# Attention's values in two passes over one bank, its sums on GpSimd, in a hybrid encoder layer

## The chip, the cores and the metric

The kernel runs on one core of one Trainium2 chip, in one launch. The metric is the device time of that launch in microseconds.

## The reference

One encoder layer is applied to two sequences of 2048 and 256 positions with the same weights. All inputs are fp32. Cut to what matters here:

```python
def encoder_layer(x, ...):
    h = rmsnorm(x, norm1_w)
    mq, mk, mv, mo, gates, aq, ak, av = jnp.split(h @ w_in, cuts, axis=-1)
    m_out = mlstm_mixer(mq, mk, mv, mo, gates, b_gates, mh_norm_w)   # 8 heads of 64, both directions
    a_out = attention_mixer(aq, ak, av, q_norm_w, k_norm_w)          # 8 query heads, 2 key/value heads
    x = x + jnp.concatenate([m_out, a_out], axis=-1) @ w_out
    u = centred_dwconv(rmsnorm(x, norm2_w) @ w_up, conv_w, conv_b)
    a, g = jnp.split(u, 2, axis=-1)
    return x + (jax.nn.silu(g) * a) @ w_down

# within attention_mixer, after the rms norms of q and k and the rotary embedding:
    def block(qi):
        s = jnp.einsum('bqhgd,bkhd->bhgqk', qi, k).astype(jnp.float32) * scale
        p = jax.nn.softmax(s, axis=-1)
        return jnp.einsum('bhgqk,bkhd->bqhgd', p.astype(v.dtype), v)
```

## The kernel before

Matrix products on fp32 data are made from fp32r products, TensorE's rounded form of fp32: an operand x is split into a high part (x rounded to fp32r) and a low part (x minus the high part, rounded again), and a product is high x high + high x low + low x high. `g.ident`, `g.identr` and `g.ones` are an identity in fp32, one in fp32r and a 128x2 block of ones.

**Stages.** `phase_a` normalises the input and projects gates, queries, keys and values of attention. `gate_math` prepares the mLSTM's gates. Then `run_both` interleaves two generators, `attention` and `mlstm`, step by step: each step yields its estimated TensorE time, and the one that is behind in its share goes next (`A_PAIR`, `A_MAX` and `A_PREP` are the estimates of attention's steps). When the mLSTM is through, the rest of attention is interleaved with `phase_c`, the output projection, and `phase_d`, the feed-forward part, follows. Within a stage a planner orders each engine's instructions by a simulated schedule and by priorities; the mLSTM's small steps have a high one. Each engine then works through its own list in order.

**Attention.** The work is cut into 36 query groups of 512 columns (four blocks of 128 queries; one head or two). 32 groups see the 2048 keys of the long sequence, that is 16 blocks of 128 keys, and 4 see the 256 keys of the short one, 2 blocks. In all there are 32 x 16 + 4 x 2 = 520 blocks of 128 keys by 512 queries. One step `kp` takes two such blocks:

- `scores`: two fp32r matmuls (lines 595 and 596) put the scores, with the query's maximum already taken off, into a PSUM bank `ps`. ScalarE takes exp twice: once rounded to fp32r into `ph` (line 599), and once in fp32 back into the bank (line 600). VectorE subtracts them into the low part `pl` (line 601).
- `maxstep`: for the next group, a matmul of queries against 512 keys into a bank `px` (line 569), of which VectorE takes the maximum per query (line 570). The banks of `ps`, `px` and a few transposes are the four buffers of the tag `sc`.
- `values`, two steps later (`PLAG`): six matmuls of line 613 add to the bank `pv`. The high values lie in a tile with 64 columns of ones beside them, so that the products of `ph` and `pl` with them leave the values on partitions 0 to 63 and the sums of the exps, 64 times over, on partitions 64 to 127. The low values lie in a tile of 64 columns, whose product with `ph` goes to partitions 0 to 63 alone.

At the end of a group `fin1` copies both halves of `pv` out with ScalarE (lines 621 and 622). The list `fins` holds what follows, of which one entry is done per step: `fin2` four times (VectorE inverts a quarter of the 64x512 sums, line 630), `fin3` (GpSimd multiplies, line 634, and issues the stores to `mix_d`), `fin4` (marks rows as ready for `phase_c`).

**What else runs on GpSimd in this stretch**, in its one queue: the mLSTM's mask selects (line 864) behind their loads (line 856), its weighted keys (line 825), the powers of its rms norms (lines 100 and 101), and in `phase_c` the sums of squares (line 1054). Other operations that the prediction names: line 849 (the mLSTM's recurrence), 904 to 921 (its outputs), 1029 (split of the mixed heads in `phase_c`), 131 and 142 (the sums of squares over partitions and their broadcast over columns, in `rstd_cols` and `rstd_rows`), and in `phase_d` 1181, 1278, 1364 and 1374 on VectorE and 1189 to 1192 on GpSimd.

Of the kernel before, what the change touches and what calls it, by code (L numbers as in the profile page):

```python
# [9 lines left out]
F32 = mybir.dt.float32  # L10
F32R = mybir.dt.float32r
AF = mybir.ActivationFunctionType
ALU = mybir.AluOpType
# [4 lines left out]
P = 128  # L18
# [6 lines left out]
HD = 64  # L25
# [32 lines left out]
DMB = 6  # L58
KWB = 2
LEAD = 1.3  # L60
A_PAIR = 2.3
A_MAX = 0.23
A_PREP = 1.0
C_MM = 1.43
# [8 lines left out]
PO = 4  # L73
PB = 4
PHB = 6
PLB = 6
PLAG = 2
ZT = 3
SG = 3
# [9 lines left out]
def f32(ap):  # L89
    return ap.bitcast(F32)  # L90
# [382 lines left out]
def attention(g, tc, s1, s2, pp):  # L473


    nc = g.nc
    sp = s1
# [13 lines left out]
    def load_kv(grp, k0, k1, after=None):  # L491

        if (grp, k0) in kv:
            return
        n = k1 - k0
        sp = s2 if n == NT1 else s1
        kv[(grp, k0)] = parts = []
        for t0 in range(0, n, 4):
            m = min(4, n - t0)
            s = f"{n}_{t0}"  # L500
            kk = sp.tile([P, m * P], F32R, tag="kk" + s, name=f"kk{grp}_{s}", bufs=1)
            kl1 = sp.tile([65, m * P], F32R, tag="kl1" + s, name=f"kl1{grp}_{s}", bufs=1)
            vs = [sp.tile([P, m, P if a == 0 else HD], F32R, tag=f"v{a}" + s, name=f"v{a}{grp}_{s}", bufs=1)
                  for a in range(2)]
            c = slice((k0 + t0) * P, (k0 + t0 + m) * P)
            if after is not None:
                for t in (kk[0:1, 0:1], kk[HD:HD + 1, 0:1], kl1[0:1, 0:1], vs[0][0:1, 0, 0:1], vs[1][0:1, 0, 0:1]):
                    nc.gpsimd.tensor_copy(t, after[0:1, 0:1])
            nc.gpsimd.memset(f32(vs[0][:, :, HD:]), 1.0)
            for r in (0, HD):  # L510
                nc.gpsimd.dma_start(f32(kk[r:r + HD, :]), g.k_d[grp, 0:HD, c])
            nc.gpsimd.dma_start(f32(kl1[0:HD, :]), g.k_d[grp, HD:P, c])
            nc.gpsimd.memset(f32(kl1[64:65, :]), 1.0)
            for a in range(2):
                nc.gpsimd.dma_start(f32(vs[a][:, :, 0:HD]), g.v_d[a, grp, :, k0 + t0:k0 + t0 + m])
            parts.append((kk, kl1, vs))

    class HB:
        pass
# [1 line left out]
    def part(s):  # L521

        t, r = 0, []
        for q in s.qs:
            r.append((t, q))
            t += q[2] - q[1]
        return r
# [13 lines left out]
    def prep(n):  # L541

        s = HB()
        grp, s.qs, k0, k1 = hbs[n]
        load_q(n)
        load_q(n + 1)
        load_kv(grp, k0, k1)
        s.kv = kv[(grp, k0)]
        s.nq, s.nk = 4, k1 - k0
        s.N = s.nq * P  # L550
        s.nm = "%d_%d" % s.qs[0][0:2]
        qz = qzs.pop(n)
# [35 lines left out]
    def scores(s, kp):  # L588
        N = s.N
        parts = []  # L590
        for z in range(2):
            ps = pp.tile([P, 512], F32, tag="sc", name=f"ps{s.nm}_{kp}_{z}")[:, 0:N]
            kk, kl1, _ = s.kv[kp // 2]
            kc = (2 * kp + z) % 4 * P
            nc.tensor.matmul(ps, kk[:, kc:kc + P], s.qq[:, 0:N], start=True, stop=False)  # L595
            nc.tensor.matmul(ps, kl1[:, kc:kc + P], s.qm[:, 0:N], start=False, stop=True)  # L596
            ph, pl = (sp.tile([P, 512], F32R, tag=t, name=f"{t}{s.nm}_{kp}_{z}", bufs=n)[:, 0:N]
                      for t, n in (("ph", PHB), ("pl", PLB)))
            nc.scalar.activation(ph, ps, AF.Exp)  # L599
            nc.scalar.activation(ps, ps, AF.Exp)  # L600
            nc.vector.tensor_tensor(pl, ps, f32(ph), ALU.subtract)  # L601
            parts.append((ph, pl))
        return parts

    def values(s, kp, parts):

        N = s.N
        if kp == 0:
            s.pv = pp.tile([P, 512], F32, tag="pv", name="pv" + s.nm, bufs=1)
        vs = [[v[:, (2 * kp + z) % 4, :] for v in s.kv[kp // 2][2]] for z in range(2)]  # L610
        todo = [(vs[z][k], parts[z][0]) for z in range(2) for k in range(2)] + [(vs[z][0], parts[z][1]) for z in range(2)]
        for k, (v, p) in enumerate(todo):
            nc.tensor.matmul(s.pv[0:HD if k in (1, 3) else P, 0:N], v, p, start=(kp == 0 and k == 0),  # L613
                             stop=(2 * kp + 2 == s.nk and k == 5))

    def fin1(s):

        N = s.N
        s.o1 = sp.tile([HD, 512], F32, tag="o1", name="o1" + s.nm, bufs=2)
        s.rs = sp.tile([HD, 512], F32, tag="rs", name="rs" + s.nm, bufs=1)  # L620
        nc.scalar.activation(s.o1[:, 0:N], s.pv[0:HD, 0:N], AF.Copy)
        nc.scalar.activation(s.rs[:, 0:N], s.pv[HD:P, 0:N], AF.Copy)
        s.left = list(range(0, N, P))

    def fin2(s):

        if s.left:
            r = s.rs[:, s.left[0]:s.left[0] + P]
            s.left.pop(0)
            nc.vector.reciprocal(r, r)  # L630

    def fin3(s):
        N = s.N
        nc.gpsimd.tensor_tensor(s.o1[:, 0:N], s.o1[:, 0:N], s.rs[:, 0:N], ALU.mult)
        for t0, (h, q0, q1) in part(s):
            r0 = HD * (h % 2)
            nc.gpsimd.dma_start(g.mix_d[q0 // 2:q1 // 2, r0:r0 + HD, 4 + h // 2].rearrange("n p t -> p n t"),
                                s.o1[:, t0 * P:(t0 + q1 - q0) * P].rearrange("p (n t) -> p n t", t=BT))
# [15 lines left out]
    prep2a(cur)  # L654
    prep2b(cur)
    load_kv(0, 0, NT1, cur.m4)
    todo, fins = [], []

    def value():

        s, kp, parts = todo.pop(0)
        values(s, kp, parts)
        if kp == s.nk // 2 - 1:
            while fins:
                fins.pop(0)()
            fin1(s)
            fins.extend([lambda: fin2(s)] * 4 + [lambda: fin3(s), lambda: fin4(s)])

    for n in range(len(hbs)):
        nxt = prep(n + 1) if n + 1 < len(hbs) else None  # L670
# [3 lines left out]
        for kp in range(nkp):  # L674
            todo.append((cur, kp, scores(cur, kp)))
            yield 0.4 * A_PAIR
            if ready:
                prep2b(ready)
                ready = None
            if nxt is not None and nxt.todo:  # L680
                if n == len(hbs) // 2 - 1:

                    k = 2 * (kp - 2) - (nxt.nq * nxt.nsp - len(nxt.todo))
                else:
                    k = -(-len(nxt.todo) // max(nkp - kp - (MXZ if g.alone else MXE), 1))
                for i in range(k):
                    maxstep(nxt)
                    if i % 2:
                        yield 2 * A_MAX
                if not nxt.todo:  # L690
                    prep2a(nxt)
                    ready = nxt
            if len(todo) > PLAG:
                value()
                yield 0.6 * A_PAIR
            for _ in range(1 if kp < nkp - 1 else 2):
                if fins:
                    fins.pop(0)()
# [9 lines left out]
    while todo:  # L708
        yield A_PAIR
        value()  # L710
# [873 lines left out]
```

## Time and profile before

| | |
|---|---|
| device time, median of 3 runs | 3426.95 us (3423.08 to 3429.48) |
| the profiled execution, first to last instruction | 3427.2 us |
| TensorE busy | 3329.3 us, 97% |
| VectorE busy | 2677.3 us, 78% |
| ScalarE busy | 1931.2 us, 56% |
| GpSimd busy | 1120.9 us, 33% |

The profiled execution's time is its span; nothing is recorded outside it, and it stands 0.25 us over the median of the runs. In the profile's lines PE is TensorE's matmuls, PEld its weight loads, DVE VectorE, ACT ScalarE and POOL GpSimd; a line number such as L601 is one of the kernel before.

How to read them: a group of instructions is given as line, engine, operation, output<-inputs, shapes and count, then the busy time in us and the mean of one in ns, then the idle time of that engine just before them and what ended it. An answer in order of time gives start and length in us, then engine, line and operation; several like instructions in a row are merged into one line (x4). A row of a stretch of time gives its bounds and length, then the busy time of each engine with its count in brackets, TensorE's granted clock, the share of the DMA engines and GB/s; asked for one source line, it has that line's busy time alone. A row of waits names who waited, for whom, the sum in us, how often, and the longest.

### The profile page before, as it was taken

The numbers are of one execution on the slowest core, as the hardware profiler recorded it, in microseconds if no ns is written. First come the engines' busy times: TensorE is split into PE (matmuls) and PEld (weight loads), VectorE is DVE, ScalarE is ACT, GpSimd is POOL, SyncE is SP. The second block draws the span as 40 slices with busy tenths as digits, with TensorE's granted clock in tenths as the row PEclk, the third lists the DMA queues.
The fourth block names the chain that finished last, engine by engine and source line by source line (L and its number), as shares of the span: only waits on it lengthen the run. The fifth ranks groups of instructions, "written<-read, shape, count | busy, mean of one in ns | idle before, by whom it ended". The sixth has DMA issues, their size and how long they took to land. (4 is left out here: it accounts for less than half of the span.)

```text
span 3427.2 us, 55596 instructions
## 1 busy us (share of the span) xinstructions
PE 3329.3 (97%) x20058; PEld 3098.4 (90%) x20058; DVE 2677.3 (78%) x4654; ACT 1931.2 (56%) x4329; POOL 1120.9 (33%) x1328
## 2 busy tenths in 40 slices
PE   7989999999999999899999999999999999999998
PEld 6878888888888888688899999999999999999998
DVE  6885687777768788967767878789888888888776
ACT  4536666666666767655544444446444446555554
POOL 6653132213232323211244333226233224322222
PEclk9999999999999999999999999999999999999999
DMA  6765342333345444422365232223323213421221
GB/s 220 243 203 159 89 140 86 115 123 98 108 131 160 143 123 139 145 77 94 101 216 198 81 105 87 68 80 133 129 94 103 72 59 128 140 74 62 69 74 50
DMA packets 254756, 404.27 MB, mean 118 GB/s; under 512 B 32112, under 2 KB 156816, under 8 KB 254480
## 3 DMA queue, kind: packets, MB, share of 16 engines
q1 hardware_dynamic: 226576, 358.23, 32.7%
q0 software_dynamic: 11344, 33.04, 3.6%
q10 hardware_dynamic: 16560, 9.44, 0.9%
q8 instruction: 158, 2.59, 0.3%
q14 instruction: 118, 0.97, 0.1%
HBM read 316.73 MB, written 83.90 MB: 117 GB/s over the span
## 5 line engine op out<-in xcount | busy, mean ns | idle before, releaser
L1322 PE MATMUL pd<-act,wd 128*128 128x384 f32 (+1 forms) x3120 | 593.4, 336 | 23.9 <-DVE acc L1324 12.6
L1322 PEld LDWEIGHTS pd<-act,wd 128*128 128x128 f32 x3120 | 539.6, 188 | 32.6 <-DVE acc L1324 18.1
L601 DVE TENSOR_TENSOR pl<-ps,ph 128x512 fp32r<-128x512 f32 x520 | 352.7, 683 | 181.5 <-ACT ps L600 173.4
L1184 PE MATMUL pa<-nt,wut 128*128 128x386 f32 (+2 forms) x2376 | 454.3, 339 | 0.0
L599 ACT ACTIVATE ph<-ps 128x512 fp32r<-128x512 f32 x520 | 309.4, 595 | 243.5 <-PE ps L596 239.5
L1184 PEld LDWEIGHTS pa<-nt,wut 128*128 128x128 f32 x2376 | 421.6, 190 | 0.3 <-ACT u L1200 0.3
L570 DVE TENSOR_REDUCE mx<-px 128x1 f32<-128x512 f32 (+1 forms) x528 | 345.5, 670 | 74.4 <-PE px L569 72.4
L1278 DVE SCALAR_TENSOR_TENSOR y<-u,cw,y 128x768 f32<-128x768 f32 (+1 forms) x264 | 315.6, 1196 | 36.4 <-ACT y L1271 29.3
L1189 POOL TENSOR_TENSOR tw<-ru 128x512 f32<-128x512 f32 x66 | 94.1, 1425 | 732.5 <-DMA ru<-w_up 558.5
L613 PE MATMUL pv<-ph,v 128*128 128x512 f32 (+1 forms) x1040 | 319.4, 401 | 1.0 <-ACT ph L599 0.8
L600 ACT ACTIVATE ps<-ps 128x512 f32<-128x512 f32 x520 | 310.3, 597 | 0.0
L1200 ACT ACTIVATE u<-pa 128x386 f32<-128x386 f32 (+2 forms) x264 | 128.3, 486 | 320.9 <-PE pa L1184 320.7
L1324 DVE TENSOR_TENSOR acc<-pd,acc 128x384 f32<-128x384 f32 (+1 forms) x544 | 280.3, 535 | 35.5 <-PE pd L1322 34.1
L1041 PEld LDWEIGHTS po<-cmx,wo 128*128 128x128 f32 x1728 | 220.7, 191 | 8.2 <-DVE mmx L931 0.6
L1041 PE MATMUL po<-cmx,wo 128*128 128x256 f32 x1728 | 224.2, 284 | 0.4 <-DVE mmx L931 0.4
L595 PE MATMUL ps<-qq,kk 128*128 128x512 f32 x520 | 215.5, 416 | 4.2 <-DVE mx L570 2.4
L569 PE MATMUL px<-kk,qq 128*128 128x512 f32 (+1 forms) x528 | 202.8, 413 | 6.0 <-DVE mx L570 2.9
L596 PE MATMUL ps<-qm,kl 65*128 65x512 f32 x520 | 206.7, 399 | 0.0
L759 PE MATMUL mj<-mn,wm 128*128 128x256 f32 x1296 | 203.0, 289 | 2.8 <-ACT og L773 1.9
L759 PEld LDWEIGHTS mj<-mn,wm 128*128 128x128 f32 x1296 | 187.1, 193 | 19.8 <-ACT og L773 2.0
L769 PEld LDWEIGHTS mv<-wm,mn 128*128 128x128 f32 x1296 | 182.8, 190 | 18.4 <-ACT qb L765 2.5
L769 PE MATMUL mv<-wm,mn 128*128 128x256 f32 x1296 | 196.5, 285 | 1.0 <-ACT qb L765 0.9
(288 smaller groups left out, 7266.6 us busy)
## 6 DMA issues: line engine op xcount, KB each, us to landing
ru<-w_up SPq DMA_DIRECT2D x132, 512.0 KB, 3.4
mn<-n_d SPq DMA_DIRECT2D x216, 256.0 KB, 3.4
rd<-w_down SPq DMA_DIRECT2D x66, 512.0 KB, 3.6
n_d<-n1T SPq DMA_DIRECT2D x18, 1024.0 KB, 5.6
dm<-nm_d POOLq DMA_DIRECT2D x72, 256.0 KB, 4.1
mjn<-n_d SPq DMA_DIRECT2D x72, 256.0 KB, 3.3
mvn<-n_d SPq DMA_DIRECT2D x72, 256.0 KB, 3.1
q_d<-qz SPq DMA_DIRECT2D x18, 512.0 KB, 3.7
```

The source lines that it names most:

```text
L570: nc.vector.tensor_reduce(s.mx[:, t, z0:z0 + 1], ps[:, 0:w], AX.X, ALU.max)
L599: nc.scalar.activation(ph, ps, AF.Exp)
L600: nc.scalar.activation(ps, ps, AF.Exp)
L601: nc.vector.tensor_tensor(pl, ps, f32(ph), ALU.subtract)
L613: nc.tensor.matmul(s.pv[0:HD if k in (1, 3) else P, 0:N], v, p, start=(kp == 0 and k == 0), stop=(2 * kp + 2 == s.nk and k == 5))
L759: nc.tensor.matmul(pj[:, o], s.w[c][:, a, o * P:(o + 1) * P], nT[c][:, :, h, :], start=(c + o + k == 0), stop=(c == NCC - 1 and k == 2 and ...
L769: nc.tensor.matmul(pv[:, o], nT[c][:, o, a, :], s.w[c][:, h, 256:512], start=(c + o + k == 0), stop=(c == NCC - 1 and k == 2 and o == 1))
L1041: nc.tensor.matmul(po[:, o], wo[z // 2][c][:, a, n], mx[c][:, h, :], start=(c == 0 and k == 0), stop=(c == NCC - 1 and k == 2))
L1184: nc.tensor.matmul(p, w[:, aa, c, :], ops[k][:, c, bb, 0:n], start=c == 0 and i == 0 and not add, stop=c == NCC // 2 - 1 and i == 2, skip_ ...
L1278: nc.vector.scalar_tensor_tensor(y[:, s:e], u[:, s + k:e + k], cw[:, k, jj:jj + 1], y[:, s:e], ALU.mult, ALU.add)
L1322: nc.tensor.matmul(po, wds[j][c // 4][:, aa, c % 4 * P:(c % 4 + 1) * P], acts[j][:, bb, z0:z1], start=(j == 0 and k == 0), stop=(j == len( ...
L1324: nc.vector.tensor_tensor(accs[c][:, z0:z1], po, accs[c][:, z0:z1], ALU.add)
```

## The change

The low values move beside the high ones, into the place of the ones: one tile `v` with the high values in columns 64 to 127 and the low ones in columns 0 to 63. A block's values are then two matmuls, of `ph` and of `pl`, both with all 128 columns: the bank gets the products with the low values on partitions 0 to 63 and with the high values on 64 to 127, and `fin1` adds the two halves (a copy of one on ScalarE, an addition on VectorE). The product low x low is now included.

The sums of the exps are no longer made on TensorE. The fp32 exp goes to a tile `pf` in SBUF (three buffers) instead of back into the bank; VectorE subtracts from there, and GpSimd adds the blocks of a group up in `acc`. At the end, `fin1b` sums `acc` over partitions with four fp32 matmuls by two columns of ones, so that the sums stand as columns, and inverts these; `fin2` broadcasts them back to rows with four fp32 matmuls through the identity, and ScalarE copies them out. The buffers of `pl` go from 6 to 5 and those of `o1` from 2 to 1, and the estimate `A_PAIR` from 2.3 to 1.9.

```diff
-A_PAIR = 2.3
+A_PAIR = 1.9
-PLB = 6
+PLB = 5
+PFB = 3
...
-            vs = [sp.tile([P, m, P if a == 0 else HD], F32R, tag=f"v{a}" + s, name=f"v{a}{grp}_{s}", bufs=1)
-                  for a in range(2)]
+            v = sp.tile([P, m, P], F32R, tag="v" + s, name=f"v{grp}_{s}", bufs=1)
...
-            nc.gpsimd.memset(f32(vs[0][:, :, HD:]), 1.0)
...
-                nc.gpsimd.dma_start(f32(vs[a][:, :, 0:HD]), g.v_d[a, grp, :, k0 + t0:k0 + t0 + m])
+                nc.gpsimd.dma_start(f32(v[:, :, (1 - a) * HD:(2 - a) * HD]), g.v_d[a, grp, :, k0 + t0:k0 + t0 + m])
... scores
             nc.scalar.activation(ph, ps, AF.Exp)
-            nc.scalar.activation(ps, ps, AF.Exp)
-            nc.vector.tensor_tensor(pl, ps, f32(ph), ALU.subtract)
+            pf = sp.tile([P, 512], F32, tag="pf", name=f"pf{s.nm}_{kp}_{z}", bufs=PFB)[:, 0:N]
+            nc.scalar.activation(pf, ps, AF.Exp)
+            nc.vector.tensor_tensor(pl, pf, f32(ph), ALU.subtract)
+            if kp + z == 0:
+                s.pf0 = pf
+            elif kp == 0:
+                s.acc = sp.tile([P, 512], F32, tag="pacc", name="pacc" + s.nm, bufs=2)[:, 0:N]
+                nc.gpsimd.tensor_tensor(s.acc, s.pf0, pf, ALU.add)
+            else:
+                nc.gpsimd.tensor_tensor(s.acc, s.acc, pf, ALU.add)
... values
-        vs = [[v[:, (2 * kp + z) % 4, :] for v in s.kv[kp // 2][2]] for z in range(2)]
-        todo = [(vs[z][k], parts[z][0]) for z in range(2) for k in range(2)] + [(vs[z][0], parts[z][1]) for z in range(2)]
-        for k, (v, p) in enumerate(todo):
-            nc.tensor.matmul(s.pv[0:HD if k in (1, 3) else P, 0:N], v, p, start=(kp == 0 and k == 0),
-                             stop=(2 * kp + 2 == s.nk and k == 5))
+        for z in range(2):
+            v = s.kv[kp // 2][2][:, (2 * kp + z) % 4]
+            for k in range(2):
+                nc.tensor.matmul(s.pv, v, parts[z][k], start=kp + z + k == 0,
+                                 stop=2 * kp + 2 == s.nk and z + k == 2)
... fin1
-        s.o1 = sp.tile([HD, 512], F32, tag="o1", name="o1" + s.nm, bufs=2)
-        s.rs = sp.tile([HD, 512], F32, tag="rs", name="rs" + s.nm, bufs=1)
-        nc.scalar.activation(s.o1[:, 0:N], s.pv[0:HD, 0:N], AF.Copy)
-        nc.scalar.activation(s.rs[:, 0:N], s.pv[HD:P, 0:N], AF.Copy)
-        s.left = list(range(0, N, P))
+        s.o1 = sp.tile([HD, 512], F32, tag="o1", name="o1" + s.nm, bufs=1)
+        o1 = s.o1[:, 0:N]
+        nc.scalar.activation(o1, s.pv[HD:P], AF.Copy)
+        nc.vector.tensor_tensor(o1, s.pv[0:HD], o1, ALU.add)
+
+    def fin1b(s):
+
+        pt = pp.tile([P, 512], F32, tag="sc", name="pt" + s.nm)
+        s.r4 = sp.tile([P, 4, 2], F32, tag="r4", name="r4" + s.nm, bufs=2)
+        for t in range(s.nq):
+            nc.tensor.matmul(pt[:, 2 * t:2 * t + 2], s.acc[:, t * P:(t + 1) * P], g.ones[:, 0:2], start=True, stop=True)
+        nc.vector.reciprocal(s.r4, pt[:, 0:8].rearrange("p (t k) -> p t k", k=2))
 
     def fin2(s):
 
-        if s.left:
-            r = s.rs[:, s.left[0]:s.left[0] + P]
-            s.left.pop(0)
-            nc.vector.reciprocal(r, r)
+        N = s.N
+        pb = pp.tile([P, 512], F32, tag="sc", name="pb" + s.nm)
+        for t in range(s.nq):
+            nc.tensor.matmul(pb[:, t * P:(t + 1) * P], s.r4[:, t, 0:1].to_broadcast([P, P]), g.ident, start=True, stop=True)
+        s.rs = s.acc[0:HD]
+        nc.scalar.activation(s.rs, pb[0:HD, 0:N], AF.Copy)
... in value(), after fin1
-            fins.extend([lambda: fin2(s)] * 4 + [lambda: fin3(s), lambda: fin4(s)])
+            fins.extend([lambda: None, lambda: fin1b(s), lambda: fin2(s), lambda: fin3(s), lambda: fin4(s)])
```

More of the change, by code (lines that the diff above doesn't have):

```diff
@@ L502, in load_kv @@
             kl1 = sp.tile([65, m * P], F32R, tag="kl1" + s, name=f"kl1{grp}_{s}", bufs=1)
-            vs = [sp.tile([P, m, P if a == 0 else HD], F32R, tag=f"v{a}" + s, name=f"v{a}{grp}_{s}", bufs=1)
-                  for a in range(2)]
+            v = sp.tile([P, m, P], F32R, tag="v" + s, name=f"v{grp}_{s}", bufs=1)
             c = slice((k0 + t0) * P, (k0 + t0 + m) * P)
             if after is not None:
-                for t in (kk[0:1, 0:1], kk[HD:HD + 1, 0:1], kl1[0:1, 0:1], vs[0][0:1, 0, 0:1], vs[1][0:1, 0, 0:1]):
+                for t in (kk[0:1, 0:1], kk[HD:HD + 1, 0:1], kl1[0:1, 0:1], v[0:1, 0, 0:1], v[0:1, 0, HD:HD + 1]):
                     nc.gpsimd.tensor_copy(t, after[0:1, 0:1])
-            nc.gpsimd.memset(f32(vs[0][:, :, HD:]), 1.0)
             for r in (0, HD):
@@ L514, in load_kv @@
             for a in range(2):
-                nc.gpsimd.dma_start(f32(vs[a][:, :, 0:HD]), g.v_d[a, grp, :, k0 + t0:k0 + t0 + m])
-            parts.append((kk, kl1, vs))
+                nc.gpsimd.dma_start(f32(v[:, :, (1 - a) * HD:(2 - a) * HD]), g.v_d[a, grp, :, k0 + t0:k0 + t0 + m])
+            parts.append((kk, kl1, v))
     class HB:
@@ L591, in scores @@
         for z in range(2):
+            ph, pl = (sp.tile([P, 512], F32R, tag=t, name=f"{t}{s.nm}_{kp}_{z}", bufs=n)[:, 0:N]
+                      for t, n in (("ph", PHB), ("pl", PLB)))
+            parts.append((ph, pl))
             ps = pp.tile([P, 512], F32, tag="sc", name=f"ps{s.nm}_{kp}_{z}")[:, 0:N]
@@ L596, in scores @@
             nc.tensor.matmul(ps, kl1[:, kc:kc + P], s.qm[:, 0:N], start=False, stop=True)
-            ph, pl = (sp.tile([P, 512], F32R, tag=t, name=f"{t}{s.nm}_{kp}_{z}", bufs=n)[:, 0:N]
-                      for t, n in (("ph", PHB), ("pl", PLB)))
             nc.scalar.activation(ph, ps, AF.Exp)
-            nc.scalar.activation(ps, ps, AF.Exp)
-            nc.vector.tensor_tensor(pl, ps, f32(ph), ALU.subtract)
-            parts.append((ph, pl))
+            pf = sp.tile([P, 512], F32, tag="pf", name=f"pf{s.nm}_{kp}_{z}", bufs=PFB)[:, 0:N]
[8 more added lines that the diff above has]
+                nc.gpsimd.tensor_tensor(s.acc, s.acc, pf, ALU.add)
         return parts
@@ L608, in values @@
         if kp == 0:
-            s.pv = pp.tile([P, 512], F32, tag="pv", name="pv" + s.nm, bufs=1)
-        vs = [[v[:, (2 * kp + z) % 4, :] for v in s.kv[kp // 2][2]] for z in range(2)]
-        todo = [(vs[z][k], parts[z][0]) for z in range(2) for k in range(2)] + [(vs[z][0], parts[z][1]) for z in range(2)]
-        for k, (v, p) in enumerate(todo):
-            nc.tensor.matmul(s.pv[0:HD if k in (1, 3) else P, 0:N], v, p, start=(kp == 0 and k == 0),
-                             stop=(2 * kp + 2 == s.nk and k == 5))
+            s.pv = pp.tile([P, 512], F32, tag="pv", name="pv" + s.nm, bufs=1)[:, 0:N]
+        for z in range(2):
[3 more added lines that the diff above has]
+                                 stop=2 * kp + 2 == s.nk and z + k == 2)
     def fin1(s):
         N = s.N
-        s.o1 = sp.tile([HD, 512], F32, tag="o1", name="o1" + s.nm, bufs=2)
-        s.rs = sp.tile([HD, 512], F32, tag="rs", name="rs" + s.nm, bufs=1)
-        nc.scalar.activation(s.o1[:, 0:N], s.pv[0:HD, 0:N], AF.Copy)
-        nc.scalar.activation(s.rs[:, 0:N], s.pv[HD:P, 0:N], AF.Copy)
-        s.left = list(range(0, N, P))
-    def fin2(s):
-        if s.left:
-            r = s.rs[:, s.left[0]:s.left[0] + P]
-            s.left.pop(0)
-            nc.vector.reciprocal(r, r)
+        s.o1 = sp.tile([HD, 512], F32, tag="o1", name="o1" + s.nm, bufs=1)
[8 more added lines that the diff above has]
+        nc.vector.reciprocal(s.r4, pt[:, 0:8].rearrange("p (t k) -> p t k", k=2))
+    def fin2(s):
+        N = s.N
[4 more added lines that the diff above has]
+        nc.scalar.activation(s.rs, pb[0:HD, 0:N], AF.Copy)
     def fin3(s):
```

## The prediction

> **What bounds the kernel now.** I read the page first, then the busy times by stage, then the instructions of TensorE in order of time, then the groups kept apart by shape, and last the waits.
>
> ```profile
> span 3427.2 us, 55596 instructions
> ```
>
> The profiled execution spans 3427.2 us, against a median of 3426.95 for the runs; the sum is made against the span, and what lies around it is taken as nothing. Attention runs from about 290 to 1790 us. From 290 to 1440 it shares the core with the mLSTM, from 1440 to 1790 with the output projection.
>
> ```profile
> core 0: us, PE busy (x) PEld busy (x) DVE busy (x) ACT busy (x) POOL busy (x), PEclk, DMA share, GB/s
> 290.00:1440.00 1150.00, 1135.12 (x7128) 988.82 (x7126) 882.05 (x1949) 776.64 (x2092) 308.33 (x621) 0.99 0.41 120
> 1440.00:1790.00 350.00, 344.25 (x2199) 303.74 (x2200) 242.97 (x412) 186.61 (x368) 76.37 (x77) 0.99 0.39 126
> ```
>
> TensorE is busy 98.7% and 98.4% of the two parts. Busy time includes the matmuls' latency, so what counts is the distance between starts:
>
> ```profile
> 1618.33 0.39 PE L596 MATMUL ps<-qm,kl 65*128 65x512 f32 x1
> 1618.56 0.40 PE L595 MATMUL ps<-qq,kk 128*128 128x512 f32 x1
> 1618.79 0.40 PE L596 MATMUL ps<-qm,kl 65*128 65x512 f32 x1
> 1619.02 1.59 PE L1041 MATMUL po<-cmx,wo 128*128 128x256 f32 x12
> ```
>
> A 512-column matmul lasts 0.40 us, but the next starts 0.23 us after it. So TensorE sets the pace here, and a removed matmul of this width is worth 0.23 us, not 0.40. The reader is to see too that VectorE is second: 76.7% and 69.4% of the two parts. GpSimd stands at 27% and 22%.
>
> **The change part by part.** Attention's unit is a block of 128 keys against 512 queries, and a step takes two of them:
>
> ```profile
> 290.00:1440.00 1150.00, 272.42 (x400) 0.99 0.41 120
> 1440.00:1790.00 350.00, 77.67 (x116) 0.99 0.39 126
> ```
>
> These are the subtractions of line 601 by part, one per block: 400 and 116 blocks, 200 and 58 steps, 0.68 us each. A step takes 1150/200 = 5.75 us in the first part, 350/58 = 6.03 in the second.
>
> *Matmuls removed.* Values go from three matmuls per block to two; the one that goes is the 64-wide one:
>
> ```profile
> L613 PE MATMUL pv<-ph,v 128*64 128x512 f32 x516 | 204.7, 397 | 0.0
> ```
>
> 516 x 0.23 = 119 us less on TensorE.
>
> *Matmuls added.* Each of the 36 query groups gets four fp32 products with two columns and four broadcasts through the identity. Both forms are in the trace, at the rms sums of the output projection:
>
> ```profile
> 1612.96 0.50 PE L131 MATMUL rs_c<-ones,cacc 128*128 128x2 f32 x4
> 1613.32 0.48 PE L595 MATMUL ps<-qq,kk 128*128 128x512 f32 x1
> ```
> ```profile
> 1616.26 0.61 PE L142 MATMUL rs_c<-ident,rcol_c 128*128 128x128 f32 x4
> 1616.62 1.17 PE L613 MATMUL pv<-ph,v 128*128 128x512 f32 x4
> ```
>
> An fp32 product is two records there (two column groups, four records), and four records push the next matmul back by 0.36 us. Sixteen records cost 1.44 us, and 36 groups 52 us. TensorE's net is -67 us, or 0.46 - 0.18 = 0.28 us a step. If nothing else bound, steps would fall to 5.47 and 5.75 us.
>
> *VectorE relieved.* The four reciprocals of a group go:
>
> ```profile
> 290.00:1440.00 1150.00, 88.63 (x104) 0.99 0.41 120
> 1440.00:1790.00 350.00, 27.02 (x32) 0.99 0.39 126
> ```
> ```profile
> L906 DVE RECIPROCAL dn<-dn 128x4 f32<-128x4 f32 x72 | 12.3, 170 | 0.9
> ```
>
> These are line 630's. In their place each group has an addition out of PSUM (0.68, as line 601's, an upper bound for 64 partitions) and one narrow reciprocal (0.17). First part: 882.05 - 88.63 + 26 x 0.85 = 815.5 us, 4.08 a step. Second: 242.97 - 27.02 + 8 x 0.85 = 222.8, 3.84 a step.
>
> *GpSimd loaded.* 32 long groups add 15 times and 4 short ones once, 484 additions of 128x512:
>
> ```profile
> L1054 POOL TENSOR_TENSOR cacc<-cacc,csq 128x512 f32<-128x512 f32 x21 | 27.8, 1322 | 133.3 <-ACT csq L1052 132.1 <-issue 1.2
> ```
>
> At the 1.29 us of an undisturbed one (the row of line 1191 below) that is 624 us. First part: 308.33 + 375 x 1.29 = 792 us of 1150. By throughput it fits. The additions wait for ScalarE's exp; behind them in GpSimd's order stand the mLSTM's mask selects, its weighted keys and rms powers, and the issues of its mask loads, for which ScalarE, TensorE and VectorE wait.
>
> *The new conflict.* Line 601 now reads PSUM and SBUF; after the change it reads SBUF twice, while GpSimd also reads SBUF. What happens then is in the last stage:
>
> ```profile
> 2030.43 1.02 DVE L1278 SCALAR_TENSOR_TENSOR y<-u,cw,y 128x767 f32<-128x767 f32 x1 [0.49 <-ACT y L1271]
> ```
> ```profile
> 2045.55 0.68 DVE L1374 TENSOR_TENSOR wd<-rd,wd 128x512 fp32r<-128x512 f32 x1
> 2046.15 0.95 DVE L1364 TENSOR_TENSOR act<-y,act 128x768 fp32r<-128x768 f32 x1
> 2047.02 0.68 DVE L1374 TENSOR_TENSOR wd<-rd,wd 128x512 fp32r<-128x512 f32 x1
> ```
> ```profile
> 2050.92 1.10 DVE L1181 TENSOR_TENSOR wut<-tw,wut 128x512 fp32r<-128x512 f32 x1 [2.75 <-ACT wut L1180]
> 2051.95 2.05 DVE L1278 SCALAR_TENSOR_TENSOR y<-u,cw,y 128x767 f32<-128x767 f32 x1
> ```
> ```profile
> 2045.63 3.22 POOL L1189 TENSOR_TENSOR tw<-ru 128x512 f32<-128x512 f32 x1 [7.10 <-DMA ru<-w_up]
> ```
> ```profile
> 2050.18 1.29 POOL L1191 TENSOR_TENSOR ru<-ru,ru 128x512 f32<-128x512 f32 x1
> 2051.44 1.74 POOL L1192 TENSOR_TENSOR tw<-ru,tw 128x512 f32<-128x512 f32 x1
> ```
>
> Line 1181's subtraction takes 0.68 us alone (672/682/2030 ns is its spread). Here it starts under GpSimd's addition, which ends at 2051.47, and ends at 2052.02, 0.55 us later: it did nothing until the addition was through, and only some 0.13 us of start-up overlapped. Line 1278's operation then takes 2.05 instead of 1.02. And GpSimd takes 3.22 us for 1.29 us of work behind three operations of VectorE in a row. The two engines exclude each other when VectorE has two SBUF inputs.
>
> ```profile
> L1181 DVE TENSOR_TENSOR wu<-ru,wu x132: 672/682/2030, 1782.7 to 3354.6; 128x512 fp32r<-128x512 f32 x132
> ```
>
> [...]
>
> A subtraction and an addition of the same block are released by the same exp, so they meet every time. A subtraction's wait lies between 0 (it goes first, as the three in a row did) and 1.29 - 0.13 = 1.16 us (a whole addition ahead). The two contended rows waited 0.42 and 1.03; I take half an addition, 0.58, 1.16 a step. The other VectorE operations with two SBUF inputs in the first part are the mLSTM's:
>
> ```profile
> L849 DVE SCALAR_TENSOR_TENSOR C<-C,dec,C 128x65 f32<-128x65 f32 x128 | 37.9, 300 | 16.0 <-ACT C L841 14.0
> L907 DVE TENSOR_TENSOR s<-s,dn 128x256 f32<-128x256 f32 x72 | 30.9, 429 | 1.2
> L919 DVE TENSOR_TENSOR hh<-hh,mr 128x128 f32<-128x128 f32 x72 | 24.9, 346 | 29.3 <-POOL mr L101 28.3 <-ACT ps L600 0.5
> L910 DVE TENSOR_TENSOR hh<-s 128x128 f32<-128x128 f32 x72 | 23.8, 331 | 0.7
> L921 DVE SCALAR_TENSOR_TENSOR hh<-ogr,hh 128x128 f32<-128x128 f32 x54 | 21.9, 406 | 0.5
> L904 DVE SCALAR_TENSOR_TENSOR dn<-s 128x4 f32<-128x4 f32 x72 | 14.5, 201 | 0.5
> L905 DVE TENSOR_TENSOR dn<-dn,tm 128x4 f32<-128x4 f32 x72 | 13.1, 182 | 0.9
> L1029 DVE TENSOR_TENSOR cmx<-cmx 128x256 fp32r<-128x256 f32 x64 | 34.4, 574 | 6.0 <-ACT cmx L1028 5.7
> ```
>
> 542 of them, 2.7 a step; line 1029 is the second part's, 1.1 a step. The additions hold 2 x 1.16 of a 5.5 us step, 42%; an operation that comes at random waits 0.42 x 0.58 = 0.24 us: 0.65 and 0.26 us a step.
>
> VectorE's step is then 4.08 + 1.16 + 0.65 = 5.89 us in the first part and 3.84 + 1.16 + 0.26 = 5.26 in the second. If it runs as full as TensorE does now (98.7%), the first part's step is 5.97 us: VectorE bounds it, 0.22 us over the 5.75 of now, +44 us in 200 steps. In the second part TensorE still bounds with 5.75, -0.28 x 58 = -16 us. Sum: **3427 + 44 - 16 = 3455 us**.
>
> *At nothing:* ScalarE's second exp goes to SBUF with the same width, and its copies per group stay two. The bank of the scores comes free before the subtraction instead of after it, a gain of a few us at most:
>
> ```profile
> PE px L569 <- DVE pl L601: 2.1, 3, 1.1
> PE ps L595 <- DVE pl L601: 1.6, 1, 1.6
> ```
>
> That is all that TensorE waits for line 601 now. The single pv bank is freed by a copy and then an addition on VectorE; the next group's first values come a step later, which covers it unless VectorE is over 4 us behind. Three buffers for the SBUF exps are covered while an addition ends within about a step of its exp; if not, ScalarE stops, and with it the mLSTM's exps and copies. The column sums are asked for a step after the group's end and the inverse a step later still, so TensorE doesn't wait for them. The planner's 1.9 for 2.3 scales both sides of its comparison alike.
>
> **The rivals.** *VectorE goes first and TensorE still bounds: 3427 - 67 = 3360 us.* It needs VectorE's first-part step under 5.47 x 0.987 = 5.40, so waits of the subtractions under 5.40 - 4.08 - 0.65 = 0.67 a step, 0.33 each. For it: the 3.22 us row, where VectorE in a row keeps GpSimd out. Against it: the additions are nearly twice as long as the subtractions, and the 2.05 us row. This is the one that ends faster; chance 0.28, and 0.06 that it comes half way.
>
> *GpSimd becomes the bound: 3541 us.* It works in order, and now stands still for others:
>
> ```profile
> POOL mr L100 <- ACT s L913: 268.0, 58, 17.0
> ```
>
> With 792/200 = 3.96 us a step and two waits of 0.55 for subtractions it needs 5.06, 1012 us; were the 268 us of waits for the mLSTM's squares kept on top, the first part would take 1280 us, +130, less 16. Against it: those waits are mostly idleness that the additions would fill. Chance 0.17.
>
> *The two balance*, within 0.2% (7 us, about what this kernel's runs can tell from no change): 0.08.
>
> **How the numbers follow.** VectorE as the bound has 0.41, so slower is 0.41 + 0.17 = 0.58, faster 0.28 + 0.06 = 0.34, the same 0.08. The likeliest case's own range is 3435 to 3520. If every subtraction waited a whole addition, the first part's step would be 7.14 us and the time about 3730, which I leave out, with the last of the 3360 case: 3370 to 3560.
>
> **What would show it.** Line 613: two groups of 516 in the stage. The subtraction's mean would rise from 0.68 us to about 1.26 (at 0.7 to 1.0 the first rival is right); the maximum's reduction in line 570 should stay as it is, since it reads PSUM. VectorE over 95% busy from 290 to 1440 with TensorE's starts no longer 0.23 apart, waiting for maxima and low parts, would be the forecast; GpSimd over 90% and ScalarE idle before its exp for GpSimd's additions, the second rival; TensorE at 98% in a stage of about 1430 us, the first. [...]

## The result and the profile after

The changed kernel takes 3584.25 us in the median (3580.54 to 3590.81), the kernel before 3426.34 beside it: a ratio of 1.0463, 95% interval 1.0448 to 1.0478. It is slower, as forecast, but by 158 us where 28 were forecast, and outside the range. The profiled execution spans 3584.0 us.

The time is lost in the stage that was changed. The busy times of its three parts follow, with the columns as before the change (TensorE, its weight loads, VectorE, ScalarE, GpSimd, each with its count, then TensorE's granted clock). 1510 to 1610 is where the mLSTM ends and the groups of the short sequence pass.

```profile
290.00:1510.00 1220.00, 1125.17 (x7003) 986.97 (x7002) 1079.47 (x1807) 748.57 (x2035) 848.72 (x967) 0.97 0.37 112
1510.00:1610.00 100.00, 76.86 (x349) 60.33 (x348) 73.69 (x136) 47.19 (x104) 44.72 (x40) 0.79 0.24 73
1610.00:1950.00 340.00, 317.99 (x2070) 288.59 (x2069) 262.00 (x355) 164.57 (x327) 230.26 (x177) 0.96 0.35 115
```

The subtractions (line 602 now, VectorE's busy time with its count) by part tell the steps:

```profile
290.00:1510.00 1220.00, 395.54 (x386) 0.97 0.37 112
1510.00:1610.00 100.00, 25.94 (x25) 0.79 0.24 73
1610.00:1950.00 340.00, 123.37 (x105) 0.96 0.35 115
```

The same numbers of blocks in the kernel before (line 601):

```profile
290.00:1383.00 1093.00, 262.97 (x386) 1.00 0.41 121
1383.00:1473.00 90.00, 16.83 (x25) 0.91 0.44 129
1473.00:1790.00 317.00, 70.28 (x105) 0.99 0.37 120
```

The first 386 blocks are 193 steps of 6.32 us where they were 5.66, and lose 127 us. The next 25 lose 10, the last 105 lose 23. VectorE stands at 88.5% in the first part, GpSimd at 70%, and TensorE is at 92.2%: none is full. The feed-forward stage, from 1950 on, takes 1634 us against 1637.

The groups of the stage, 290 to 1950, apart by shape (busy time, mean in ns, then idle time and what ended it):

```profile
L609 POOL TENSOR_TENSOR pacc<-pacc,pf 128x512 f32<-128x512 f32 x448 | 653.7, 1459 | 211.4 <-ACT pf L601 184.2 <-ACT mkT L777 6.2 <-DVE dn L922 3.6
L602 DVE TENSOR_TENSOR pl<-pf,ph 128x512 fp32r<-128x512 f32 x516 | 544.8, 1067 | 94.7 <-ACT pf L601 88.4 <-issue 1.9 <-ACT qm L585 1.8
L569 DVE TENSOR_REDUCE mx<-px 128x1 f32<-128x512 f32 x496 | 323.9, 678 | 50.8 <-PE px L568 50.1
L620 PE MATMUL pv<-pl,v 128*128 128x512 f32 x516 | 222.5, 431 | 41.5 <-DVE pl L602 40.8
L865 DVE SCALAR_TENSOR_TENSOR C<-C,dec,C 128x65 f32<-128x65 f32 x128 | 80.7, 634 | 13.1 <-ACT C L857 11.3
L935 DVE TENSOR_TENSOR hh<-hh,mr 128x128 f32<-128x128 f32 x72 | 60.2, 836 | 15.1 <-POOL mr L102 14.5 <-ACT pf L601 0.6
L923 DVE TENSOR_TENSOR s<-s,dn 128x256 f32<-128x256 f32 x72 | 45.3, 629 | 1.1
L926 DVE TENSOR_TENSOR hh<-s 128x128 f32<-128x128 f32 x72 | 39.7, 552 | 0.9
L920 DVE SCALAR_TENSOR_TENSOR dn<-s 128x4 f32<-128x4 f32 x72 | 39.0, 542 | 0.9
L937 DVE SCALAR_TENSOR_TENSOR hh<-ogr,hh 128x128 f32<-128x128 f32 x54 | 36.8, 681 | 0.3
L921 DVE TENSOR_TENSOR dn<-dn,tm 128x4 f32<-128x4 f32 x72 | 34.7, 482 | 1.0
```

The subtraction takes 1067 ns where it took 683, on the same data, and the mLSTM's operations on two SBUF inputs rise by 0.2 to 0.5 us each; the reduction, which reads PSUM, keeps its 678. One such wait in order of time, VectorE and GpSimd:

```profile
643.57 1.54 DVE L923 TENSOR_TENSOR s<-s,dn 128x256 f32<-128x256 f32 x1
```
```profile
643.53 1.29 POOL L609 TENSOR_TENSOR pacc<-pacc,pf 128x512 f32<-128x512 f32 x1 [2.02 <-ACT pf L601]
```

Line 923 starts 0.04 us after the addition and ends 0.29 us after it. The longest waits of the stage (who for whom, us in all, times, longest):

```profile
ACT ph L599 <- PE ps L598: 213.8, 132, 9.5
POOL pacc L609 <- ACT pf L601: 184.2, 95, 8.8
ACT s L929 <- DVE hh L926: 137.4, 59, 7.6
...
DVE pl L602 <- ACT pf L601: 88.4, 92, 3.0
PEld pv L620 <- DVE pl L602: 61.0, 65, 3.8
...
PEld px L568 <- DVE mx L569: 28.3, 38, 3.1
...
ACT pf L601 <- POOL pacc L609: 12.6, 16, 2.1
```

VectorE is late; ScalarE, in order, stands behind the mLSTM's squares for VectorE's `hh` (137 us, one wait up to 7.6); the exps come later; TensorE waits for low parts and maxima. That order of events is read from the waits; which of them sets the pace is for the runs below. And after one of its waits TensorE is slower besides:

```profile
1554.45 0.79 PE L620 MATMUL pv<-ph,v 128*128 128x512 f32 x1 [6.52 <-DVE o L629]
1555.05 0.63 PE L620 MATMUL pv<-pl,v 128*128 128x512 f32 x1
1555.47 0.63 PE L620 MATMUL pv<-ph,v 128*128 128x512 f32 x1
1555.90 0.63 PE L620 MATMUL pv<-pl,v 128*128 128x512 f32 x1
...
1577.74 0.39 PE L620 MATMUL pv<-ph,v 128*128 128x512 f32 x1
1577.97 0.39 PE L620 MATMUL pv<-pl,v 128*128 128x512 f32 x1
```

After a wait of 6.5 us the starts are 0.43 us apart, about twice 0.23, and only some 20 us later they are back. The clock granted is 1.00 from 1540 to 1542, 0.50 in the wait (1548 to 1554.4), then 0.61 to 1565, 0.55 to 1576.5, and 1.00 from there to 1590; in the row of 1510 to 1610 it is 0.79. Part of it is not new: the same 25 blocks had 0.91 before.

What TensorE waits for there is the bank `pv`, and through it the single buffer of o1:

```profile
1509.61 0.63 PE L620 MATMUL pv<-pl,v 128*128 128x512 f32 x1
```
```profile
1541.22 1.27 POOL L650 TENSOR_TENSOR o<-o,pacc 64x512 f32<-64x512 f32 x1 [6.30 <-ACT pacc L646]
1544.11 1.15 POOL L653 DMA_DIRECT2D mix_d<-o  x2
1561.11 1.26 POOL L650 TENSOR_TENSOR o<-o,pacc 64x512 f32<-64x512 f32 x1 [15.85 <-ACT pacc L646]
```
```profile
1551.29 0.59 ACT L628 ACTIVATE o<-pv 64x512 f32<-64x512 f32 x1
```

The last value product of a short group starts at 1509.61, and ScalarE copies it out at 1551.29, some 41 us later. In between the group before it, which still holds o1, is multiplied and stored. VectorE's addition follows at 1553.73. GpSimd stands idle all through the 6.52 us (it is idle for 15.85 us up to 1561.11), so waits for its additions are not what holds TensorE up in them.

### The profile page after: what moved, and what is told of

Its sections match the earlier page's. It is cut to its first block, busy times and chain, and to the rows that moved or that the text cites. A ratio compares the mean times of both kernels' runs of the same rounds, so it can differ in the third digit from the quotient of the medians.

```text
span 3584.0 us, 56668 instructions
## 1 busy us (share of the span) xinstructions
PE 3368.3 (94%) x20114; PEld 3139.6 (88%) x20114; DVE 2963.9 (83%) x4582; ACT 1925.2 (54%) x4329; POOL 1838.8 (51%) x1802
## 5 line engine op out<-in xcount | busy, mean ns | idle before, releaser
L609 POOL TENSOR_TENSOR pacc<-pacc,pf 128x512 f32<-128x512 f32 x448 | 653.7, 1459 | 211.4 <-ACT pf L601 184.2
L602 DVE TENSOR_TENSOR pl<-pf,ph 128x512 fp32r<-128x512 f32 x520 | 547.7, 1064 | 94.7 <-ACT pf L601 88.4
L599 ACT ACTIVATE ph<-ps 128x512 fp32r<-128x512 f32 x520 | 309.8, 599 | 222.2 <-PE ps L598 213.8
L1294 DVE SCALAR_TENSOR_TENSOR y<-u,cw,y 128x768 f32<-128x768 f32 (+1 forms) x264 | 307.5, 1165 | 36.4 <-ACT y L1287 29.3
L601 ACT ACTIVATE pf<-ps 128x512 f32<-128x512 f32 x520 | 310.8, 600 | 20.9 <-POOL pacc L609 12.6
L620 PE MATMUL pv<-pl,v 128*128 128x512 f32 x520 | 224.1, 431 | 41.5 <-DVE pl L602 40.8
L597 PE MATMUL ps<-qq,kk 128*128 128x512 f32 x520 | 226.1, 437 | 10.3 <-DVE mx L569 9.4
L620 PE MATMUL pv<-ph,v 128*128 128x512 f32 x520 | 216.2, 416 | 17.4 <-DVE o L629 12.9
```

The costliest lines, as they stand in the source:

```text
L601: nc.scalar.activation(pf, ps, AF.Exp)
L602: nc.vector.tensor_tensor(pl, pf, f32(ph), ALU.subtract)
L609: nc.gpsimd.tensor_tensor(s.acc, s.acc, pf, ALU.add)
L620: nc.tensor.matmul(s.pv, v, parts[z][k], start=kp + z + k == 0, stop=2 * kp + 2 == s.nk and z + k == 2)
L1294: nc.vector.scalar_tensor_tensor(y[:, s:e], u[:, s + k:e + k], cw[:, k, jj:jj + 1], y[:, s:e], ALU.mult, ALU.add)
```

## The experiments

Theory 1 was the forecast's: VectorE's subtraction, with two inputs from SBUF, and GpSimd's addition exclude each other. Rivals: GpSimd's time in itself, since the mLSTM's steps stand in its queue behind the additions (theory 2), and the new end of a group, with one o1 (theory 3).

**The exp back in PSUM, sums of the high parts.** GpSimd adds as much as before, but the subtraction has one SBUF input again.

```diff
-            pf = sp.tile([P, 512], F32, tag="pf", ...)
-            nc.scalar.activation(pf, ps, AF.Exp)
-            nc.vector.tensor_tensor(pl, pf, f32(ph), ALU.subtract)
+            nc.scalar.activation(ps, ps, AF.Exp)
+            nc.vector.tensor_tensor(pl, ps, f32(ph), ALU.subtract)
+            pf = f32(ph)
```

> The changed kernel, but the fp32 exp goes back into the PSUM bank, VectorE subtracts from there as before the change, and GpSimd adds the high parts ph instead of fp32 exps (so the sums are those of the rounded exps). GpSimd has the same 484 additions of the same size, TensorE the same matmuls; only the subtraction has one SBUF input again. Theory 1 (the shared SBUF access: subtraction and addition exclude each other): the subtraction's mean falls from 1067 ns to about 690, VectorE in the stretch 290 to 1510 falls from 88% to under 82%, and the time to 3370 to 3430, as TensorE bounds again; the mLSTM's small operations still wait. Theory 2 (GpSimd's load in itself: the mLSTM's steps stand in its queue behind the additions): the time stays over 3530. Theory 3 (the group's end: pv is freed through a copy and an addition, one o1): no change, 3570 to 3600.

Measured: 3493.67 us, ratio 1.0182 (1.0161 to 1.0202). Its groups from 290 to 1500:

```profile
L609 POOL TENSOR_TENSOR pacc<-pacc,ph 128x512 f32<-128x512 f32 x341 | 443.4, 1301 | 154.2 <-ACT ph L599 134.9 <-DVE s L923 4.3 <-DVE dn L920 1.2
L601 DVE TENSOR_TENSOR pl<-ps,ph 128x512 fp32r<-128x512 f32 x395 | 268.8, 684 | 129.4 <-ACT ps L600 123.4 <-PE pv L620 4.3 <-PE ps L598 0.3
L865 DVE SCALAR_TENSOR_TENSOR C<-C,dec,C 128x65 f32<-128x65 f32 x128 | 71.7, 565 | 12.8 <-ACT C L857 10.9
```

The subtraction is back at 684 ns, the addition at 1301, and 90 us of the 158 are gone. Theory 3 alone is out. But the time lies between the other two: theory 1 expected 3430 at most, theory 2 over 3530. More than the subtraction's conflict is at work, and line 865 (the recurrence, 300 ns before) still waits.

**No additions.** The first addition of a group and one scalar addition stay, so the sums are not the softmax's.

```diff
                 nc.gpsimd.tensor_tensor(s.acc, s.pf0, pf, ALU.add)
-            else:
-                nc.gpsimd.tensor_tensor(s.acc, s.acc, pf, ALU.add)
+                nc.gpsimd.tensor_scalar(s.acc, s.acc, 1.0, None, ALU.add)
```

> The changed kernel without GpSimd's additions but the first of each group (one scalar addition of 1.0 takes the place of all the others, so the sums are not the softmax's). Subtraction still from two SBUF inputs. Theory 1 and theory 2 both expect the whole loss back, 3350 to 3400; the difference to the run with sums of the high parts is what the remaining conflict with the mLSTM's small operations and GpSimd's queue cost: under 30 us by theory 1, over 100 by theory 2. Theory 3: 3550 to 3600.

Measured: 3380.13 us, ratio 0.9854 (0.9839 to 0.9868). So the additions cost 204 us, and what the change gains without them is 50 us against the 3430 of the kernel before in these runs; the forecast's sum for TensorE was 67. The run with sums of the high parts stands 114 us above this one. Theory 1 expected under 30 there, theory 2 over 100: on this point theory 1 missed, and the memsets below ask why.

**A third exp.** The subtraction reads a third exp from PSUM, GpSimd the fp32 exp in SBUF.

```diff
+            nc.scalar.activation(ps, ps, AF.Exp)
-            nc.vector.tensor_tensor(pl, pf, f32(ph), ALU.subtract)
+            nc.vector.tensor_tensor(pl, ps, f32(ph), ALU.subtract)
```

> The changed kernel with a third exp on ScalarE, back into the PSUM bank, from which VectorE subtracts; GpSimd adds the fp32 exps from SBUF as changed. The conflict of subtraction and addition goes as in the run with sums of the high parts, at the price of 520 more exps of 0.6 us (0.5 us each back to back) on ScalarE, which was busy 61% of 290 to 1510. Theory 1: 3380 to 3460, ScalarE at 80%. Theory 2: over 3540. Theory 3: 3570 to 3620.

Measured: 3542.74 us, ratio 1.0326 (1.031 to 1.0341). By the numbers that is theory 2's case (over 3540), if only just, and 83 us over theory 1's. Taking the subtraction out of the conflict gains 41 us even with 520 more exps on ScalarE, which is then busy 77% of 290 to 1360; with the price of these exps unknown the run decides nothing more.

**TensorE's third matmul put back.**

```diff
                 nc.tensor.matmul(s.pv, v, parts[z][k], ...)
+                if k == 0:
+                    nc.tensor.matmul(s.pv[0:HD], v[:, 0:HD], parts[z][0], start=False, stop=False)
```

> The changed kernel with a third matmul per block put back on TensorE (high exps by the low values once more, 64 wide, so the low values count twice): 520 x 0.23 = 119 us of TensorE's work. If VectorE and GpSimd set the pace and TensorE waits (theory 1 or 2), little of it shows: 3580 to 3640. If TensorE is still what bounds, with waits on top (theory 3), all of it does: about 3700.

Measured: 3583.8 us, ratio 1.0451 (1.0434 to 1.0469). 119 us of TensorE's work change nothing. Its first part:

```profile
290.00:1450.00 1160.00, 1110.70 (x6898) 960.63 (x6897) 1004.65 (x1649) 716.26 (x1910) 821.23 (x908) 0.99 0.35 103
```

TensorE fills its waits with the matmuls, its clock is at 0.99 instead of 0.97, and the time is the same. So TensorE doesn't set the pace of the changed kernel, and its lowered clock there is not the cause of the loss.

**Memsets in place of the additions**, on the run without additions:

```diff
+            elif kp:
+                nc.gpsimd.memset(pf, 0.0)
+                nc.gpsimd.memset(pf, 0.0)
+                nc.gpsimd.memset(pf[:, 0:256], 0.0)
```

> The run without additions, with three memsets of 512, 512 and 256 columns per block in their place (from the third block of a group on), over the SBUF exp after VectorE has read it: about as much GpSimd time per block as an addition, 1.3 us, in the same queue beside the mLSTM's steps, but nothing read from SBUF; the sums are not the softmax's. If what remains of the loss after the subtraction's conflict (from 3380 to 3494 us) is the shared SBUF access of the mLSTM's small VectorE operations, this runs like the kernel without additions, 3370 to 3410, and those operations keep their short times (hh under 420 ns, C about 320). If it is GpSimd's queue, in which the mLSTM's steps stand behind the additions, it runs at 3450 to 3520 with the small operations short all the same.

Measured: 3417.19 us, ratio 0.9966 (0.9956 to 0.9976). From 290 to 1500:

```profile
L602 DVE TENSOR_TENSOR pl<-pf,ph 128x512 fp32r<-128x512 f32 x420 | 303.8, 730 | 155.5 <-ACT pf L601 149.1 <-PE pv L623 3.0 <-ACT qm L585 1.0
L606 POOL MEMSET pf<- 128x512 f32 x364 | 190.4, 527 | 153.3 <-DVE pl L602 149.0 <-DVE dn L925 1.0
L607 POOL MEMSET pf<- 128x512 f32 x364 | 189.4, 527 | 8.1
L608 POOL MEMSET pf<- 128x256 f32 x364 | 110.8, 311 | 8.2
L868 DVE SCALAR_TENSOR_TENSOR C<-C,dec,C 128x65 f32<-128x65 f32 x128 | 42.8, 337 | 24.7 <-ACT C L860 22.8
```

This is the run that tells the theories apart. GpSimd spends 1.37 us a block, more than the 1.30 of an addition in the run with sums of the high parts, in the same queue; the subtraction reads SBUF twice; and it takes 730 ns, line 868 (the recurrence) takes 337. GpSimd's time in its queue costs 3417 - 3380 = 37 us (theory 2), the reading of SBUF 3584 - 3417 = 167 us (theory 1). The time lies 7 us over the 3410 expected for the shared access alone, and 33 under the 3450 expected for the queue. One difference remains: the memsets come after the subtraction, the additions after the exp. But they do meet the subtractions of other blocks, and those keep their time:

```profile
703.46 0.52 POOL L606 MEMSET pf<- 128x512 f32 x1
```
```profile
703.52 0.68 DVE L602 TENSOR_TENSOR pl<-pf,ph 128x512 fp32r<-128x512 f32 x1
```

**The new operand alone, in the kernel before.** Exp to SBUF and subtraction from there; two buffers of pf, five of pl, one o1; no additions, values as before.

```diff
-            nc.scalar.activation(ps, ps, AF.Exp)
-            nc.vector.tensor_tensor(pl, ps, f32(ph), ALU.subtract)
+            nc.scalar.activation(pf, ps, AF.Exp)
+            nc.vector.tensor_tensor(pl, pf, f32(ph), ALU.subtract)
```

> The kernel before with one part of the change alone: the fp32 exp goes to SBUF (two buffers; those of pl 5 for 6, of o1 1 for 2, to make room) and VectorE subtracts from there; values, sums and GpSimd as before. Theory of the shared access: GpSimd is busy 27% here, so the subtraction's mean rises only from 683 to about 735 ns, VectorE to 78% of the stretch, and the time stays within 3420 to 3450. If SBUF operands or the buffers' number cost by themselves, 3480 or more.

Measured: 3442.3 us, ratio 1.0044 (1.003 to 1.0058). With GpSimd's work of before (308 us of 290 to 1440 there, 27%), reading SBUF twice cost 15 us, in which the fewer buffers are included. The loss needs both parts of the change.

**The planner's estimate**, `A_PAIR` at 2.3 in the changed kernel.

> The changed kernel with the estimate A_PAIR at 2.3 again. It shifts how the planner mixes attention with the mLSTM. If the loss came from the mix of the work and not from waits, this recovers a large part, under 3500; by the theory of the shared access it changes little, 3560 to 3610.

Measured: 3566.29 us, ratio 1.0405 (1.0389 to 1.042). 18 us, small beside the loss.

**Buffers**, on the run with sums of the high parts: two o1 and six pl (the `bufs=2` and `PLB = 6` of before).

> The run with sums of the high parts, with the two buffers of o1 and the six of pl that the kernel before had. If the single o1 and the five pl, which the short groups wait for around the change of the key head, cost by themselves, 15 to 40 us less than the run with sums of the high parts (3494), 3455 to 3480; if not, within 10 us of it.

Measured: 3453.92 us, ratio 1.0079 (1.0064 to 1.0094): some 40 us less, so the buffers cost. Each by itself, and o1 in the changed kernel:

> The run with sums of the high parts, with two buffers of o1 and five of pl. If the single o1 is what costs (a group's end waits for the stores of the group before, and pv with it), nearly all of the 41 us comes back here: 3450 to 3465. If it is the fifth and sixth pl, 3485 to 3500.

Measured: 3458.6 us, ratio 1.0095 (1.008 to 1.011).

> The run with sums of the high parts, with one o1 and six buffers of pl. If pl is what costs (VectorE, running late, waits for TensorE to release a low part), 3450 to 3465; if the single o1, 3485 to 3500.

Measured: 3472.85 us, ratio 1.0135 (1.012 to 1.015).

> The changed kernel with two o1, for which the SBUF exps go from three buffers to two. If the single o1 costs here what it may cost with sums of the high parts, 3540 to 3560; if the shared access hides it, 3570 to 3600; if two SBUF exps are too few, over 3600.

Measured: 3602.11 us, ratio 1.0507 (1.049 to 1.0525). With the subtraction out of the conflict the second o1 is worth about 35 us and the sixth pl about 21, not the one or the other as I had put it, and together some 40. These are rough: the runs with sums of the high parts alone reach from 3482 to 3499. Part of the o1's price is the wait seen above: ScalarE's copies of the two short groups start 51.7 us apart with one o1 (1427.76 and 1479.41) and 5.6 us apart with two (1416.41 and 1422.04). In the changed kernel the second o1, paid for with a buffer of pf, gains nothing; whether pf at two took the gain away stays open.

**From there down to the kernel before?** Three more on the run with two o1 and six pl. First the mLSTM's outputs in PSUM, so that lines 902 to 910 conflict no more:

```diff
-        nc.vector.tensor_tensor(s1, pN, s1, ALU.add)
+        nc.vector.tensor_tensor(pN[:, :, :, 0:65], pN[:, :, :, 0:65], s1, ALU.add)
...
-        nc.vector.tensor_tensor(hh, s1[:, 0, :, 0:64], s1[:, 1, :, 0:64], ALU.add)
+        nc.vector.tensor_tensor(hh, s1[:, 0, :, 0:64], pN[:, 1, :, 0:64], ALU.add)
```

> The run with sums of the high parts and two o1, and the mLSTM's outputs (lines 902 to 910 of the kernel before) worked on in the PSUM bank, so that each of these VectorE operations has one SBUF input at most (two operations more per block of 128 positions, about 0.3 us). Of 542 small operations with two SBUF inputs, 254 are left. If the additions cost what they do because these operations wait for them (one behind the other, and ScalarE's squares behind them), 25 to 50 us less than 3454: 3405 to 3430, and ScalarE's wait for hh falls from 83 us to under 50. If the queue of GpSimd is what costs, no gain; and the bank is held longer, which could cost up to 20 us.

Measured: 3453.11 us, ratio 1.0066 (1.0049 to 1.0082). Without it and with it, from 340 to 1420:

```profile
ACT s L929 <- DVE hh L926: 82.9, 51, 4.9
```
```profile
ACT s L932 <- DVE hh L929: 42.8, 26, 4.9
```

ScalarE's wait halves and the time stays; that expectation fell. The operations that are left in the conflict wait longer instead (from 290 to 1500 the recurrence 623 ns on average for 578, line 935, 938 here, 889 for 634), and the bank is held longer by two operations more. So the run shows that this rewrite gains nothing, and not what the waits cost.

The planner's estimate, and each addition cut into two of 256 columns:

> The run with sums of the high parts and two o1, with A_PAIR at 2.3. In the changed kernel this gave 18 us; if the planner's mix is worth that by itself, 3430 to 3445; if it helped only because fewer subtractions met additions, 3445 to 3460.

Measured: 3461.85 us, ratio 1.0095 (1.008 to 1.011): no gain from the estimate here.

> The run with sums of the high parts and two o1, each addition cut into two of 256 columns. The shared access is held for 0.6 us at a time instead of 1.16, but GpSimd works 0.73 x 2 = 1.46 us a block instead of 1.30. If the length of a single wait of the small operations is what costs, 10 to 30 us less than 3454; if GpSimd's total time is what costs, 10 to 30 more.

Measured: 3484.73 us, ratio 1.016 (1.0145 to 1.0175). It costs 31 us. An estimate of GpSimd's time is 1.47 us a block for 1.30, as an addition of 256 columns takes 734 ns in the kernel before (line 1304); whatever the shorter single waits gain, the time shows none of it.

> The mLSTM's outputs in PSUM, A_PAIR at 2.3 and seven buffers of ph (which the additions now hold too) together, on the run with sums of the high parts and two o1. If the gains add up, 3385 to 3420, under the kernel before; if not, 3430 to 3460.

Measured: 3455.98 us, ratio 1.0075 (1.006 to 1.009). The gains don't add up. No version with the sums on GpSimd came under the kernel before; the best stands 0.7% over it.

## Why the prediction was wrong

The mechanism and the sign held: with two SBUF inputs, beside additions that read SBUF, VectorE's subtraction grew from 683 to 1067 ns (684 with one input back in PSUM, 730 beside memsets), the reduction from PSUM did not (678), and the stage that lost is the one named. The size failed, at these steps.

*"If it runs as full as TensorE does now (98.7%)."* This step carries most of the miss. VectorE needed 1079.47/193 = 5.59 us a step, less than the 5.89 summed. Full to 98.7% that would have been a step of 5.66 us, just what these blocks took before (1093/193), and nothing would have been lost in this part. But the step took 6.32: VectorE was 88.5% full. Why it doesn't fill up is read from the waits, and no run shows it by itself: VectorE waits for the exps of a ScalarE (88.4 us) that waits for VectorE's `hh` (137.4) and for TensorE's scores (213.8), and TensorE waits for VectorE's low parts and maxima. The forecast took the busy share of one engine in the old kernel for another that stands in such a loop.

*The waits themselves.* The subtraction waits 395.54/386 - 0.68 = 0.34 us in the first part, not 0.58: 0.68 a step for 1.16. The small operations of the mLSTM wait more: the means above less those of before, by their counts, are 128 x 0.33 + 72 x (0.49 + 0.20 + 0.22 + 0.34 + 0.30) + 54 x 0.28 = 169 us, 0.88 a step for 0.65. Together 1.56 for 1.81. That the sum comes within a seventh is in part luck, since the two errors offset each other.

*The second part, -16 us.* It was to be TensorE's again. Its 130 blocks lost 33 us instead, 10 where the short groups pass and 23 after them. On the last 105 blocks VectorE has 262.00/52.5 = 4.99 us of work a step (5.26 in the sum), 77% of the time, and TensorE is at 94% (98.4% in the prediction's second part): again no engine was full.

*What was priced at nothing.* The single o1 and the fifth pl are not in the sum, and came to some 40 us where the subtraction was out of the conflict. The wait of 6.52 us above is the o1's. It is not the case that the line on pv named ("a step later, which covers it unless VectorE is over 4 us behind"): VectorE's addition came 2.4 us after ScalarE's copy, and the copy itself was late. The three buffers for the SBUF exps did hold: ScalarE waits 12.6 us for them in all.

*TensorE's gain*, -67: 50 showed in the run without additions. That run has the single o1 and the five pl too, so where the other 17 went stays open.

The second rival's number (3541) lies nearer than the forecast, but not its mechanism: GpSimd is at 70%, not over 90%, and its time alone costs 37 us.

What stays open: of the 74 us between the best version (3454) and the one without additions (3380), GpSimd's time explains about 37 by the memsets. Neither taking the small output operations out of the conflict nor cutting the additions in two won back any of the rest. Line 849's recurrence, which still waits in these (578 and 623 ns above, 300 in the kernel before), was not tried without its conflict, and the bank that the exp in PSUM holds until the subtraction was not separated from it.

## What to carry to other kernels

Before moving work to GpSimd, list VectorE's operations with two SBUF inputs in that stretch: here the subtraction's mean rose from 683 to 1067 ns beside GpSimd's additions, and those of the mLSTM's operations by 0.2 to 0.5 us. Keeping one operand of the subtraction in PSUM was 90 us better than letting the subtraction and the addition read the same tile (the sums are then those of the rounded exps). Don't count on 98% for an engine that waits for two others: here it stopped at 88%, and the engine that had been the bound had room for 119 us of work. And a buffer that is taken away to make room belongs in the sum: two of them came to some 40 us here.

## What the hardware showed beyond expectation

GpSimd's memsets, which read nothing, didn't hold VectorE up here: with 1.37 us of them per block the subtraction takes 0.73 us, with 1.46 us of additions 1.07. And TensorE, after a wait of 6.5 us, issued at half pace (0.43 us between 512-column matmuls) for about 20 us in which it still had shorter waits (up to 2.9 us), before 0.23 returned; the clock granted was 1.00 from 1540 to 1542, 0.50 in the long wait, 0.61 and 0.55 in the stretch after it, and 1.00 again from 1576.5 on.
